# A two-layer hybrid decoder trunk: causal mask added by VectorE in query rows 1 to 3, and the next layer's opening placed in the TensorE order of the last rows

## The chip, the cores and the metric

The kernel runs on one core of a Trainium2 chip. The metric is the device time of one execution in microseconds (us). TensorE (PE in the rows) multiplies matrices, VectorE (DVE) does elementwise work and reductions, ScalarE (ACT) does activations and casts, GpSimd (POOL) does small work, and SyncE (SP) issues most DMAs.

## The reference, cut to what matters

A residual stream of 512 rows by 1024 columns goes through two layers. Each layer normalises it (RMSNorm), projects it to 4376 columns, runs three parallel groups (sparse attention with 8 heads, a linear recurrence, a convolution module), and adds their joint output projection back to the stream. A last RMSNorm closes the trunk. The part of the attention that the change touches is a softmax over all keys up to the query's own row:

```python
def rms_norm(x, g):
    y = xf * lax.rsqrt(jnp.mean(xf * xf, axis=-1, keepdims=True) + EPS)
    return (y * g.astype(jnp.float32)).astype(x.dtype)
...
ms = (ok[..., None] & (tok <= t[None, None, :, None, None]))[:, :, None]
ss = jnp.where(ms, ss, NEG)
ps = jax.nn.softmax(ss, axis=-1)
...
sw = jnp.einsum('bgrqd,bgkd->bgrqk', qb, kw).astype(jnp.float32) * scale
pw = jax.nn.softmax(jnp.where(mw, sw, NEG), axis=-1)
...
x = x + mixed @ w_out[l]
return rms_norm(x, final_g)
```

With 512 rows the "selected" branch takes every valid block and the window is as long as the sequence, so both branches are a causal softmax.

## The kernel before, in words

Rows are tiled by 128 into four tiles t = 0 to 3 (query row blocks i = 0 to 3). All products are made in split form: a value is held as a high part and a low part, and a product is the sum of high by high, high by low and low by high. `cast` writes a high part on ScalarE, `lower` subtracts it from the value on VectorE (tiles `whi`, `wlo`; `H` holds the turned, normalised stream in both parts).

**Opening of a layer.** For each tile the RMSNorm (`rms_norm`, in layer 0 the steps q, c, p of `START`), the turning of the result by TensorE transposes (`turned`, L271 to L274) and the projection to values and gates (L327, 24 matmuls of 280 columns for each tile). In layer 0 the order of ScalarE and VectorE is written out by hand in `START`: q is the square sum on ScalarE, c the inverse root on VectorE and GpSimd, p a product on VectorE, t a turning, w a part of the value weights. Then 384 and more projection matmuls follow without a break (L208).

**Attention, row blocks 2, 3 and 1** (`weights_of`, `turned_weights`, `values`). For each block there are eight heads and two branches; for i = 2 and 3 one call of `weights_of` handles one head and branch, for i = 1 two heads. A call writes scores to PSUM (L779, L780), adds the mask by a third matmul of `identb` and `maskb` (L781), finds the row minimum of the negated scores on VectorE (L784), takes the exponential on ScalarE from PSUM to `P` with a row sum (L787), inverts the sum (L789), scales `P` on GpSimd (L791). `turned_weights` transposes `P` on TensorE (L798), casts it on ScalarE (L800) and takes the low part on VectorE (L801); `values` multiplies it by the values (L813). PSUM buffers: three named `ps` for scores, two named `pt` for transposes, two named `acc`. `P` has four buffers in SBUF. The order of every engine outside the manual blocks is made by a scheduler. It puts the 96 matmuls of `out_proj(X, 8, MC)` (L423 with `mch`, `mcl`), which depend on nothing in the attention, between the attention's own matmuls; they are called fillers below.

**Last rows** (`last_rows`). Row block 0 and the 96 matmuls of the last part of the output projection run on TensorE in the order of `LAST_ROWS`: s scores, t turning, c and d the compressed branch, o and v the value products, r30 for example the output rows of tile 3, column half 0, added to the stream `X` by VectorE (L425). The opening of the next layer comes after them in the program, and the scheduler fills its instructions in.

**End.** The last RMSNorm writes `o` by tile, tile 0 last and in two halves, each with its own output DMA.

Of the kernel before, what the change touches and what calls it, by code (L numbers as in the profile page):

```python
# [1 line left out]

# [45 lines left out]
def tile_hybrid_trunk(ctx, tc, x_in, positions, norm_g, w_in, b_gate, cmp_pos, cmp_w1, cmp_w2, lru_conv_w,  # L48
# [30 lines left out]
    maskb = const.tile([128, 128], BF16, name="maskb")  # L79
# [132 lines left out]
    def rsqrt(y, v4):  # L212
# [706 lines left out]
    for l in range(DEPTH):  # L919
        X = layer(l, X)  # L920
# [34 lines left out]
```

## Time and profile before

| | |
|---|---|
| median of 3 runs | 786.5 us (785.53 to 787.01) |
| the profiled execution's own time | 786.09 us |
| its span, first to last instruction | 784.3 us |
| instructions | 10943 |
| PE busy (matmul) | 755.0 us, 96% |
| DVE busy | 676.4 us, 86% |
| ACT busy | 452.1 us, 58% |
| POOL busy | 101.7 us, 13% |
| mean granted TensorE clock | 0.997 |

The span leaves 1.8 us of the execution's time outside. Busy shares are means over stages that differ; a matmul's end is modelled, so consecutive matmuls overlap in the rows and the distance from start to start is what one costs.

### The profile page before, as it was taken

How to read it: one execution, taken by the hardware profiler on the slowest of the kernel's cores; microseconds unless marked ns; L12 is line 12 of the kernel's file. 1: busy time of each engine (PE TensorE's matmuls, PEld its weight loads, DVE VectorE, ACT ScalarE, POOL GpSimd, SP SyncE). 2: the span in 40 equal slices, each digit the busy share in tenths (PEclk: the TensorE clock that was granted, in tenths of full speed). 3: DMA queues.
4: the chain of work that ended last, by engine and by line, in shares of the span. 5: the costliest groups of instructions: out<-in, count | busy, mean ns of one | idle time of the engine just before them, and what ended most of it. 6: DMA issues, size and time to landing. Idle time of an engine off the chain costs nothing.

```text
span 784.3 us, 10943 instructions
## 1 busy us (share of the span) xinstructions
PE 755.0 (96%) x3816; PEld 604.8 (77%) x3816; DVE 676.4 (86%) x1243; ACT 452.1 (58%) x889; POOL 101.7 (13%) x179
## 2 busy tenths in 40 slices
PE   6999999999999999999989999999999999999995
PEld 4988887677887777888788888776788787778874
DVE  5889999999997788978873999999999778888766
ACT  5443666784336466667642348669534466676663
POOL 2000000000001132433210000000000103434240
PEclk9999999999999999999999999999999999999998
DMA  6433285656432200103531334771854140010002
GB/s 192 155 108 107 57 223 133 167 164 222 142 128 81 81 2 1 54 1 86 169 105 54 107 89 126 188 199 32 275 165 160 53 145 17 1 55 2 1 28 107
DMA packets 68245, 82.01 MB, mean 105 GB/s; under 512 B 6601, under 2 KB 56841, under 8 KB 68190
## 3 DMA queue, kind: packets, MB, share of 16 engines
q1 hardware_dynamic: 68190, 81.31, 33.9%
q8 instruction: 30, 0.49, 0.3%
q14 instruction: 25, 0.20, 0.1%
HBM read 67.67 MB, written 4.19 MB: 92 GB/s over the span
## 4 chain that ended last, share of the span: by engine, by line
PE 78%; DVE 9%; ACT 6%; issue 4%; POOL 2%; DMA 0%; POOLq 0%; DVEq 0%; SPq 0%; ACTq 0%
PE acc L208 43%; PE acc L423 10%; PE po L813 5%; PE pt L798 3%; PE acc L718 3%; PE acc L327 3%; PE ps L779 2%; ACT P L787 2%; PE ps L780 2%; DVE wlo L153 1%; DVE cv L381 1%; PE pt L630 1%; POOL P L791 1%; ACT pt L800 1%; PE pt L735 1%
## 5 line engine op out<-in xcount | busy, mean ns | idle before, releaser
L208 PE MATMUL acc<-H,whi 128*128 128x512 f32 x1024 | 325.5, 398 | 0.0
L208 PEld LDWEIGHTS acc<-H,whi 128*128 128x128 f32 x1024 | 191.1, 188 | 47.5 <-issue 1.9
L208 PE MATMUL acc<-H,wlo 128*128 128x512 f32 x512 | 203.7, 399 | 2.1 <-DVE wlo L153 2.1
L150 ACT CAST whi<-raw 128x1024 fp32r<-128x1024 f32 x102 | 106.5, 1050 | 159.4 <-PE acc L208 130.1
L381 DVE SCALAR_TENSOR_TENSOR cv<-sg,dww,cv 128x493 f32<-128x493 f32 (+18 forms) x240 | 165.9, 737 | 0.9
L153 DVE TENSOR_TENSOR wlo<-raw,whi 128x1024 fp32r<-128x1024 f32 x102 | 124.8, 1225 | 22.1 <-ACT whi L150 21.2
L208 PEld LDWEIGHTS acc<-H,wlo 128*128 128x128 f32 x512 | 96.2, 188 | 27.3 <-DVE wlo L153 3.4
L791 POOL TENSOR_SCALAR P<-P,hm,gt 128x384 f32<-128x384 f32 (+3 forms) x128 | 81.1, 643 | 135.7 <-DVE hm L789 127.1
L787 ACT ACTIVATE P<-ps,hm 128x384 f32<-128x384 f32 (+3 forms) x128 | 67.0, 532 | 15.7 <-DVE hm L784 15.1
L801 DVE TENSOR_TENSOR pt<-pt 128x512 fp32r<-128x512 f32 (+1 forms) x88 | 54.2, 638 | 12.9 <-ACT pt L800 11.8
L784 DVE TENSOR_REDUCE hm<-ps 128x1 f32<-128x384 f32 (+3 forms) x88 | 54.8, 634 | 8.2 <-PE ps L781 4.4
L813 PE MATMUL po<-pt,vv 128*128 128x256 f32 (+1 forms) x304 | 58.0, 304 | 1.1 <-DVE pt L801 0.7
L215 POOL TENSOR_TENSOR mv<-mv,power 128x1 f32<-128x1 f32 x8 | 4.2, 544 | 418.1 <-DVE mv L680 418.1
L800 ACT CAST pt<-pt 128x512 fp32r<-128x512 f32 (+1 forms) x88 | 46.0, 548 | 21.4 <-PE pt L798 18.8
L813 PEld LDWEIGHTS po<-pt,vv 128*128 128x128 f32 x304 | 44.7, 189 | 9.8 <-ACT pt L800 4.6
L798 PE MATMUL pt<-ident,P 128*128 128x128 f32 x320 | 47.6, 275 | 1.6 <-POOL P L791 1.3
L779 PE MATMUL ps<-KH,QS 128*128 128x384 f32 (+3 forms) x128 | 45.5, 367 | 0.8 <-ACT P L787 0.6
L798 PEld LDWEIGHTS pt<-ident,P 128*128 128x128 f32 x320 | 36.9, 140 | 6.0 <-POOL P L791 4.1
L780 PE MATMUL ps<-KL,QS 128*128 128x384 f32 (+3 forms) x128 | 40.5, 328 | 0.0
L327 PE MATMUL acc<-wv,H 128*128 128x280 f32 x192 | 30.6, 313 | 2.5 <-ACT wv L150 1.5
L425 DVE TENSOR_TENSOR x<-x,acc 128x512 f32<-128x512 f32 x48 | 32.4, 677 | 0.8 <-PE acc L423 0.4
L423 PE MATMUL acc<-whi,mn 128*128 128x512 f32 x96 | 31.1, 406 | 0.0
(233 smaller groups left out, 1213.3 us busy)
## 6 DMA issues: line engine op xcount, KB each, us to landing
raw<-in_w_in_dram SPq DMA_DIRECT2D x30, 1024.0 KB
raw<-in_w_out_dram SPq DMA_DIRECT2D x12, 1024.0 KB
raw<-in_cmp_w_dram SPq DMA_DIRECT2D x8, 1024.0 KB
x<-in_x_dram SPq DMA_DIRECT2D x8, 512.0 KB
raw<-in_w_in_dram SPq DMA_DIRECT2D x4, 512.0 KB
QS<-rs SPq DMA_DIRECT2D x8, 256.0 KB
QS<-ru SPq DMA_DIRECT2D x8, 256.0 KB
KH<-rs SPq DMA_DIRECT2D x8, 256.0 KB
```

The costliest lines, as they stand in the source:

```text
L150: S.copy(out, in_)
L153: (eng or V).tensor_tensor(out, in_, hi.bitcast(F32), op=OP.subtract)
L208: PE.matmul(p, w[k], h[k], start=n == 0, stop=n == 23)
L381: V.scalar_tensor_tensor(a[:, s:], u[:, :T - s], dww[:, ct, j:j + 1], a[:, s:], op0=OP.mult, op1=OP.add)
L423: PE.matmul(p, h[:, k], w, start=m == 0, stop=m == 11)
L779: PE.matmul(sc[:, r, :], q, KH[g][:, b, :L], start=r == 0, stop=False)
L780: PE.matmul(sc[:, r, :], q, KL[g][:, b, :L], start=False, stop=False)
L784: V.tensor_reduce(hm[:, 0, :nh], sc, axis=AX.X, op=OP.min)
L787: S.activation(P[:, r * L:(r + 1) * L], sc[:, r, :], AF.Exp, scale=-1.0, bias=hm[:, 0, r:r + 1], accum_out=hm[:, 1, r:r + 1])
L791: G.tensor_scalar(P[:, r * L:(r + 1) * L], P[:, r * L:(r + 1) * L], hm[:, 2, r:r + 1], GA[i][:, h0 + r, 1 + b:2 + b], op0=OP.mult, op1=OP. ...
L798: PE.transpose(pt[:, kb, :], P[:, kb * 128:(kb + 1) * 128], ident)
L813: PE.matmul(po, v, PT[w][:, kb].rearrange("p r q -> p (r q)"), start=False, stop=last and kb == i and w == 1)
```

## The change

Three things change. In row blocks 1 to 3 the mask matmul goes, and one VectorE instruction for each head adds the mask (now a bf16 tile of 512 columns, zero but for its last 128) to the scores, writes the sum to `P` and finds the minimum; the exponential then reads `P`. Row block 0 keeps the matmul. The opening of the next layer becomes an object whose steps (L loads, W value weights, N norm, T turning, V values) stand in `LAST_ROWS`, within the hand-written TensorE order. In `START` the inverse root is cut in two (c and e), the value weights come in three loads instead of two, their parts stand earlier, and the DMA of `norm_g` moves from SP's queue to ScalarE's. In `rms_norm` the tile that comes last takes its second half first, multiplies it by the gain early on VectorE and scales it on ScalarE. The small tiles `pos` and `hid` share buffers of other tiles.

```diff
-LAST_ROWS = "s10 c s00 r30 s01 r20 d r10 t00 o0 t01 s11 v00 v01 r21 t10 t11 r31 o1 v10 v11 r11 r01 r00"
-START = "q3 c3 p30 p31 q2 t30 c2 t31 p20 w0 p21 q1 t20 c1 w1 t21 p10 q0 p11 w2 t10 c0 t11 p00 p01 t00 t01"
+LAST_ROWS = "s10 c s00 r30 s01 r20 d r10 t00 o0 t01 s11 v00 v01 r21 L N2 t10 W t11 r31 N3 o1 v10 v11 T2 r11 N1 r01 " \
+            "T3 r00 N0 V2 T1 V3 T0 V1 V0"
+START = "q3 c3 e3 p30 p31 q2 c2 w0 e2 t30 p20 t31 q1 p21 c1 w1 e1 t20 p10 t21 q0 p11 c0 w2 e0 t10 p00 t11 p01 t00 t01"
...
-    maskb = const.tile([128, 128], BF16, name="maskb")
+    mask = const.tile([128, 512], BF16, name="mask")
+    maskb = mask[:, 384:]
...
+    G.memset(mask[:, :384], 0.0)
...
-        for n in range(2):
+        for n in ((1, 0) if last else (0, 1)):
             S.activation(y[:, n], x[:, n], AF.Square, accum_out=ss[:, n:n + 1])
...
+                if last:
+                    V.tensor_tensor(y[:, 1], x[:, 1], gb[:, 1], op=OP.mult)
...
-        for n in (slice(0, 1), slice(1, 2)) if halves else (slice(0, 2),):
-            V.scalar_tensor_tensor(y[:, n], x[:, n], ss[:, 2:3], gb[:, n], op0=OP.mult, op1=OP.mult)
+        n = slice(0, 1 if last else 2)
+        V.scalar_tensor_tensor(y[:, n], x[:, n], ss[:, 2:3], gb[:, n], op0=OP.mult, op1=OP.mult)
+        if last:
+            S.activation(y[:, 1], y[:, 1], AF.Copy, scale=ss[:, 2:3])
...
+        load_x(0, X, (3,))
+        grow = pair("grow")[0:1].rearrange("p a c -> p (a c)")
+        S.dma_start(out=grow, in_=norm_g[0:1, :])
+        load_x(0, X, (2,))
+        load_wv(0, 3)
+        load_wv(3, 3)
+        load_x(0, X, (1, 0))
+        load_wv(6, 2)
+        load_bg()
...
-                    PE.matmul(sc[:, r, :], q, KL[g][:, b, :L], start=False, stop=False)
-                PE.matmul(sc[:, :, L - 128:], identb, maskb.unsqueeze(1).to_broadcast([128, nh, 128]),
-                          start=False, stop=True)
+                    PE.matmul(sc[:, r, :], q, KL[g][:, b, :L], start=False, stop=i > 0 and r == nh - 1)
                 hm = work.tile([128, 3, 4], F32, name="hm", tag="hm", bufs=8)
-                V.tensor_reduce(hm[:, 0, :nh], sc, axis=AX.X, op=OP.min)
                 P = big("P", tag="P")
+                if i == 0:
+                    PE.matmul(sc, identb, maskb.unsqueeze(1).to_broadcast([128, nh, 128]), start=False, stop=True)
+                    V.tensor_reduce(hm[:, 0, :nh], sc, axis=AX.X, op=OP.min)
                 for r in range(nh):
-                    S.activation(P[:, r * L:(r + 1) * L], sc[:, r, :], AF.Exp, scale=-1.0,
-                                 bias=hm[:, 0, r:r + 1], accum_out=hm[:, 1, r:r + 1])
+                    p = P[:, r * L:(r + 1) * L]
+                    if i:
+                        V.tensor_tensor_reduce(p, sc[:, r, :], mask[:, 512 - L:], 1.0, BIG, OP.add, OP.min,
+                                               hm[:, 0, r:r + 1])
+                    S.activation(p, p if i else sc[:, r, :], AF.Exp, scale=-1.0, bias=hm[:, 0, r:r + 1],
+                                 accum_out=hm[:, 1, r:r + 1])
...
-        last_rows(X)
-        return X
+        return X, last_rows(X)
```

**VectorE in the middle of row block 3.** `TENSOR_REDUCE hm<-ps` is the minimum of one call, `RECIPROCAL hm` its inverse row sum, `pt<-pt` the low part of a turned block. Before:

```order
452 L801 TENSOR_TENSOR pt<-pt 128x4x128
453 L789 RECIPROCAL hm<-hm 128x1
454 L784 TENSOR_REDUCE hm<-ps 128x1
455 L801 TENSOR_TENSOR pt<-pt 128x4x128 x2
456 L789 RECIPROCAL hm<-hm 128x1 x2
457 L153 TENSOR_TENSOR wlo<-raw,whi 128x1024
458 L801 TENSOR_TENSOR pt<-pt 128x4x128 x2
459 L789 RECIPROCAL hm<-hm 128x1
460 L784 TENSOR_REDUCE hm<-ps 128x1 x2
```

The same place with the change; `ISA P,hm<-ps,mask` is the new instruction, and `ISA hm` behind it brings the minimum out:

```order
474 L847 TENSOR_TENSOR pt<-pt 128x4x128
475 L835 RECIPROCAL hm<-hm 128x1
476 L831 ISA P,hm<-ps,mask 128x512
477 L831 ISA hm 128x1
478 L847 TENSOR_TENSOR pt<-pt 128x4x128 x2
479 L835 RECIPROCAL hm<-hm 128x1
480 L831 ISA P,hm<-ps,mask 128x512
481 L831 ISA hm 128x1
```

Each minimum of one instruction is now two, and the order around them is otherwise alike.

**TensorE at the end of row block 1.** `acc<-wlo,mch` is a filler, `pt<-ident,P` a transpose of row block 1's `P`, `po<-pt,vv` its value products, and the 128-column `ps` rows are row block 0's scores. The first row of each piece is the layer's last filler. Before:

```order
1455 L423 MATMUL acc<-wlo,mch 128x512
1456 L779 MATMUL ps<-KH_1075,QS_725 128x128
1457 L780 MATMUL ps<-KL_1077,QS_725 128x128
1458 L779 MATMUL ps<-KH_1075,QS_726 128x128
1459 L780 MATMUL ps<-KL_1077,QS_726 128x128
1460 L805 MATMUL po<-ct,vcz 128x512
1461 L813 MATMUL po<-pt,vv 128x256 x8
1462 L798 MATMUL pt<-ident,P 128x128
1463 L813 MATMUL po<-pt,vv 128x256
1464 L798 MATMUL pt<-ident,P 128x128 x3
```

Now:

```order
1374 L463 MATMUL acc<-wlo,mch 128x512
1375 L819 MATMUL ps<-KH_1079,QS_729 128x128
1376 L859 MATMUL po<-pt,vv 128x256 x3
1377 L844 MATMUL pt<-ident,P 128x128 x4
1378 L820 MATMUL ps<-KL_1081,QS_729 128x128
1379 L819 MATMUL ps<-KH_1079,QS_730 128x128
1380 L820 MATMUL ps<-KL_1081,QS_730 128x128
1381 L819 MATMUL ps<-KH_1079,QS_729 128x128
1382 L844 MATMUL pt<-ident,P 128x128 x4
```

The last filler now stands ahead of 12 transposes of `P` (two groups of four are shown, a third follows six rows later) where 4 were left before.

**TensorE between the two layers.** `acc<-whi,mn` and `acc<-wlo,mn` are the last output rows (r00), `pt<-ident,hnat` transposes of the next layer's normalised stream, `acc<-wv,H` its value products. Before:

```order
1614 L423 MATMUL acc<-wlo,mn_3534 128x512
1615 L271 MATMUL pt<-ident,hnat 128x128 x6
1616 L327 MATMUL acc<-wv,H_3868 128x280
1617 L271 MATMUL pt<-ident,hnat 128x128 x4
1618 L327 MATMUL acc<-wv,H_3870 128x280
1619 L327 MATMUL acc<-wv,H_3868 128x280
1620 L271 MATMUL pt<-ident,hnat 128x128 x4
```

Now the transposes of tiles 2 and 3 stand ahead of r00, and 24 value products come directly behind it, with tile 1's transposes after them:

```order
1533 L463 MATMUL acc<-wlo,mn_3506 128x512
1534 L307 MATMUL acc<-wv,H_3508 128x280
1535 L307 MATMUL acc<-wv,H_3510 128x280
1536 L307 MATMUL acc<-wv,H_3508 128x280 x2
1537 L307 MATMUL acc<-wv,H_3510 128x280
1538 L307 MATMUL acc<-wv,H_3508 128x280 x2
```

Transposes of one tile and value products of another now alternate in whole blocks of 8 and 24 (V2, T1, V3, T0, V1, V0), where the two were mixed row by row.

## Rows read from the trace of the kernel before

**Rows 1.** The page's chain of work that ended last, by engine.

```profile
PE 78%; DVE 9%; ACT 6%; issue 4%; POOL 2%; DMA 0%; POOLq 0%; DVEq 0%; SPq 0%; ACTq 0%
```

**Rows 2.** Stretches: length, each engine's busy us (instructions), TensorE clock, DMA share, GB/s.

```profile
5.93:27.92 21.99, 17.72 (x107) 16.40 (x107) 17.15 (x44) 13.65 (x24) 2.29 (x4) 1.00 0.65 206
266.00:362.00 96.00, 93.87 (x588) 75.59 (x588) 79.84 (x185) 65.74 (x175) 34.46 (x51) 1.00 0.07 21
393.12:414.06 20.94, 18.61 (x142) 17.33 (x140) 13.66 (x32) 9.75 (x21) 2.04 (x4) 1.00 0.25 79
```

**Rows 3.** Chain in order of time: start us, length us, what.

```profile
31.59 89.79 PE acc L208 x384
...
329.80 0.87 PE pt L798 x8
...
405.37 8.16 PE acc L327 x63
414.12 89.79 PE acc L208 x384
```

**Rows 4.** TensorE's timeline in row block 3: start us, length us, instruction.

```profile
318.84 0.23 PE L781 MATMUL ps<-maskb,identb 128*128 128x128 bf16 x1
318.88 0.48 PE L779 MATMUL ps<-KH,QS 128*128 128x512 f32 x1
319.19 0.28 PE L813 MATMUL po<-pt,vv 128*128 128x256 f32 x1
```

**Rows 5.** Groups by line and shape, whole run: count | busy us, mean ns | idle before.

```profile
L801 DVE TENSOR_TENSOR pt<-pt 128x512 fp32r<-128x512 f32 x56 | 37.3, 687 | 7.8 <-ACT pt L800 7.3
L787 ACT ACTIVATION_READ_ACCUMULATOR P<-ps,hm 128x1 f32 x128 | 26.2, 205 | 0.0
L784 DVE TENSOR_REDUCE hm<-ps 128x1 f32<-128x512 f32 x32 | 21.3, 682 | 4.8 <-PE ps L781 2.6 <-PE acc L423 1.9
L784 DVE TENSOR_REDUCE hm<-ps 128x2 f32<-128x512 f32 x16 | 10.8, 683 | 0.4 <-PE ps L781 0.4
L545 DVE TENSOR_TENSOR_SCAN xc<-xc,rg 128x512 f32<-128x512 f32 x8 | 9.6, 1222 | 0.0
...
L789 DVE RECIPROCAL hm<-hm 128x1 f32<-128x1 f32 x64 | 9.2, 153 | 1.7 <-ACT P L787 1.5
...
L332 DVE TENSOR_TENSOR vv<-acc,vv 128x256 fp32r<-128x256 f32 x8 | 3.4, 420 | 3.1 <-ACT vv L331 3.1
```

**Rows 6.** Two such inversions back to back, VectorE's timeline in row block 3.

```profile
323.58 0.21 DVE L789 RECIPROCAL hm<-hm 128x1 f32<-128x1 f32 x2
```

**Rows 7.** TensorE's timeline at the border of the layers.

```profile
386.00 0.62 PE L423 MATMUL acc<-whi,mn 128*128 128x512 f32 x2
...
396.23 0.40 PE L327 MATMUL acc<-wv,H 128*128 128x280 f32 x1 [0.89 <-ACT H L273]
397.88 0.66 PE L271 MATMUL pt<-ident,hnat 128*128 128x128 f32 x4 [1.25 <-DVE H L274]
```

**Rows 8.** VectorE's timeline there: tile 0's last addition and its norm.

```profile
395.40 0.68 DVE L425 TENSOR_TENSOR x<-x,acc 128x512 f32<-128x512 f32 x1
...
400.73 0.15 DVE L228 SCALAR_TENSOR_TENSOR ss<-ss 128x1 f32<-128x1 f32 x1
```

**Rows 9.** The start, timeline: DMA issue of x on SP's queue, tile 0's last low parts.

```profile
1.20 0.83 SPq L111 DMA_DIRECT2D x<-in_x_dram  x2
...
26.54 1.38 DVE L274 TENSOR_TENSOR H<-pt,H 128x512 fp32r<-128x512 f32 x2
```

**Rows 10.** Groups of VectorE by line from 5.9 to 28 us.

```profile
L217 DVE SCALAR_TENSOR_TENSOR nw<-ss,nw 128x1 f32<-128x1 f32 x4 | 0.9, 220 | 1.4 <-POOL ss L215 1.4
```

**Rows 11.** The end, VectorE's timeline for tile 0.

```profile
778.46 0.15 DVE L227 TENSOR_SCALAR ss<-ss 128x1 f32<-128x1 f32 x1 [0.79 <-ACT o L225]
...
779.93 1.42 DVE L231 SCALAR_TENSOR_TENSOR o<-x,ss,g 128x512 f32<-128x512 f32 x2
```

More of the change, by code (lines that the diff above doesn't have):

```diff
@@ L1 @@
 from contextlib import ExitStack
+from types import SimpleNamespace
 import concourse.bass as bass
@@ L253, in chan, with layer @@
+    def layer(l, X, o):
+        Hh, Hl, VV, GT = o.Hh, o.Hl, o.VV, o.GT
         def chan(name, src2d, n):
@@ L261, in chan @@
             return t
-        H2 = [[quad(f"H{w}{a}") for a in range(2)] for w in range(2)]
-        Hh, Hl = [[H2[w][k // 4][:, k % 4, :] for k in range(8)] for w in range(2)]
-        WV = [None] * 8
-        def turned(t, h, n):
-            p = psum.tile([128, 4, 128], F32, name="pt", tag="tr", bufs=2)
-            for k in range(4):
-                PE.transpose(p[:, k, :], h[:, n, k * 128:(k + 1) * 128], ident)
-            sl = slice(t * 128, (t + 1) * 128)
-            S.copy(H2[0][n][:, :, sl], p)
-            V.tensor_tensor(H2[1][n][:, :, sl], p, H2[0][n][:, :, sl].bitcast(F32), op=OP.subtract)
@@ L287, in layer @@
-        if l == 0:
-            hs, ss = {}, {}
-            gp = [psum.tile([128, 512], F32, name="acc", tag="ps", bufs=3) for n in range(2)]
-            for n in range(2):
-                PE.matmul(gp[n], one, grow[:, n * 512:(n + 1) * 512], start=True, stop=True)
-            def squares(t):
-                hs[t] = pair("hnat")
-                ss[t] = work.tile([128, 4], F32, name="ss", tag="ss", bufs=4)
-                S.activation(hs[t], X[t], AF.Square, accum_out=ss[t][:, 0:1])
-            def chain(t):
-                V.tensor_scalar(ss[t][:, 3:4], ss[t][:, 0:1], 4.0 / DM, 4.0 * EPS, op0=OP.mult, op1=OP.add)
-                rsqrt(ss[t][:, 2:3], ss[t][:, 3:4])
-            def product(t, n):
-                V.scalar_tensor_tensor(hs[t][:, n], X[t][:, n], ss[t][:, 2:3], gp[n], op0=OP.mult, op1=OP.mult)
-            steps = dict(q=squares, c=chain, p=product, t=lambda t, n: turned(t, hs[t], n), w=value_weights)
-            with tc.manual_schedule(engines={mybir.EngineType.Activation, mybir.EngineType.DVE}):
-                for step in START.split():
-                    steps[step[0]](*map(int, step[1:]))
-        else:
-            for j in range(3):
-                value_weights(j)
-            for t in (2, 3, 1, 0):
-                SP.dma_start(out=saved[t], in_=X[t])
-                h = rms_norm(X[t], gb, "hnat", t == 0)
-                for n in range(2):
-                    turned(t, h, n)
@@ L589, in do_prep @@
         def do_prep(c):
-            pos = work.tile([16, 128], F32, name="pos", tag="pos", bufs=1)
+            pos = work.tile([16, 128], F32, name="pos", tag="oe", bufs=1)
             SP.dma_start(out=pos, in_=cmp_pos[l, c].rearrange("(j s) d -> j (s d)", s=2))
@@ L637, in do_main @@
                           stop=True)
-            hid = work.tile([128, 2, 64], F32, name="hid", tag="hid", bufs=1)
+            hid = work.tile([128, 2, 64], F32, name="hid", tag="m")
             S.activation(hid, ph, AF.Tanh, scale=0.5)
@@ L884, in last_rows @@
                     steps = dict(s=soft, t=turn, c=comp, d=turn_comp, o=open_po, v=vals, r=rows)
+                    if nxt:
+                        steps |= nxt.steps
                     for step in LAST_ROWS.split():
-                        steps[step[0]](*map(int, step[1:]))
+                        if step[0] in steps:
+                            steps[step[0]](*map(int, step[1:]))
+                return nxt
             return last_rows
@@ L914, in layer @@
         out_proj(X, 8, MC)
-        last_rows(X)
-        return X
+        return X, last_rows(X)
     X = [None] * 4
+    o = opening(0, X)
     for l in range(DEPTH):
-        X = layer(l, X)
+        X, o = layer(l, X, o)
     gb = load_g(final_g)
```

135 lines of the change are left out of this document (90 added, 45 removed).

## The prediction

> **What bounds the kernel now.** I read the chain of waits first: three quarters and more of what ended last is TensorE's own work [rows 1]. So time can come from TensorE work that goes away, or from stretches in which it waits. I then read the windows, and they show three such places [rows 2]. From 5.93 to 27.92 us, the opening of layer 0, VectorE is busy 17.15 of 21.99 us: neither engine is full, each waits for the other. From 266 to 362 us, row blocks 2, 3 and 1 of layer 0, TensorE is busy 93.87 of 96.00 us and VectorE 79.84. From 393.12 to 414.06 us, the border of the layers, neither is full. Everything between (the long runs of L208 [rows 3]) is a stream of matmuls at 89.79 / 384 = 0.234 us each, which the change doesn't touch: what is won ahead of it is passed on whole, since layer 1's first run, with no opening of layer 0 behind it, takes the same 89.79 us.
>
> **The attention stage, what goes.** Each call of `weights_of` in row blocks 1 to 3 loses a mask matmul: 16 + 16 + 8 = 40 a layer. Its price is read from starts: the mask matmul is followed after 0.04 us by the next score matmul, which then holds the one after it off for 0.31 us [rows 4], where 0.234 is the rule [rows 3]. So 0.04 + 0.08 = 0.12 us a call, 40 x 0.12 = 4.8 us of TensorE a layer. [...]
>
> **What comes in its place.** VectorE's minimum of one call (682 ns for 512 columns) becomes an instruction over the same columns with a PSUM and an SBUF source, whose nearest row is the low part of L801, 687 ns [rows 5]: no difference. In row block 1 one minimum over two heads (683 ns) becomes two of 256 columns, nearest row 420 ns: 8 x (0.840 - 0.683) = 1.3 us a layer, with the small differences 1.4. Then there is the instruction that brings each minimum out, 16 + 16 + 16 = 48 a layer, which no row of VectorE shows. Below: the second of two inversions back to back adds 0.21 - 0.153 = 0.06 us [rows 5, 6]. Above: ScalarE's own read of an accumulator, 205 ns [rows 5]. I take 0.12, between the two, because the new one can't start before the sum behind it is complete, so it hides less than an independent inversion. That makes 1.4 + 48 x 0.12 = 7.2 us of VectorE a layer (4.3 to 11.2).
>
> [...]
>
> What lies beside it: the stage's TensorE need falls from 96.0 to 91.2 us. VectorE's sum rises from 79.84 to 87.0, 95% of that. At 83% its lateness cost TensorE the 2.1 us that it stood idle. At 95%, in one fixed order, with only three score buffers, two transpose buffers and four `P`, more of the chain minimum, exponential, inversion, scaling, transpose, low part comes late. One place shows it: the last filler now stands ahead of 12 transposes of row block 1 instead of 4, so two more groups end without cover. Such a group costs VectorE a low part of 0.687 and TensorE only 0.87 / 2 = 0.435 for four transposes [rows 3, 5]; with the cast between them I price the two at 1 us each less what overlaps, 1.5 us. For the rest of the stage I take another 1.6. Net 4.8 - 3.1 = 1.7 us a layer, 3.4 in both. For the other parts of a call I put nothing: the exponential reads SBUF instead of PSUM on an engine busy 65.74 of 96 us [rows 2], and scores' PSUM buffers come free earlier, by about an exponential.
>
> **The border of the layers.** From 386.00 (r11) [rows 7] to the first projection matmul at 414.12 [rows 3] there are 28.12 us. The work in it: 36 output matmuls at 0.234 (8.4), 30 transposes at 0.87 / 8 = 0.109 (3.3), 96 value products at 8.16 / 63 = 0.130 (12.5), 8 narrow transposes at no more than 0.109 (0.9): 25.0 us. So 3.1 us are waiting, of which the two waits named in the rows (0.89 and 1.25) are the largest part [rows 7]; they end with VectorE's low part and ScalarE's cast of a turned tile. In the new order each turning has a block of other matmuls behind it: T2 has r11 and r01 (24 x 0.234 = 5.6 us), T3 has r00, T1 has V3 (24 x 0.130 = 3.1). What is late next is tile 0's norm. Before, VectorE added its last rows at 395.40 and came to its first norm step at 400.73 [rows 8], held off by other tiles' work in its queue. Now 24 + 24 products and T1's 8 transposes, 7.1 us, lie between r00 and T0, and VectorE's order puts two weight low parts and one low part of tile 1 in between; I count about 6 us for the norm, so the cover holds by 1 us. The steps' DMAs (L) stand on SP's queue where they stood. I take 2.7 us, between 1.2 (one wait stays) and 3.1.
>
> **The start.** The first x is issued at 1.20, behind the DMA of `norm_g`, and one issue takes 0.83 / 2 = 0.4 us [rows 9]; that DMA moves to another queue: 0.4 us earlier. Cutting c in two puts other work into three of four waits for GpSimd's root, 1.4 x 3 / 4 = 1.0 us [rows 10]. Of VectorE's remaining idle time (4.84 - 1.0 = 3.8 [rows 2]) I let the new order recover 1.7, nearly half. VectorE then ends tile 0's low parts 3.1 us before 27.92 [rows 9]. But 48 value products now stand behind tile 0's transposes instead of 34, 14 x 0.130 = 1.8 us. Net 1.3 us; from 0.4 (only the issue) to 0.4 + 4.84 - 1.8 = 3.4. The memset of the wider mask is hidden: GpSimd has nothing due until the first root at 6 us.
>
> **The end.** Tile 0's two halves stand one behind the other on VectorE, 1.42 us [rows 11]; one goes to ScalarE, 0.7 us, and one small step of 0.15 leaves the chain. The two output DMAs still are issued one after the other, so I take 0.7, between 0.4 and 0.9.
>
> **Sum.** 3.4 + 2.7 + 1.3 + 0.7 = 8.1 us off the profiled execution's 786.09: 778.0 us. That execution lies 0.4 us under the median of the runs, so the median may come out as much later. 0.2% (1.6 us) is about what a measurement of this kernel can tell from no change.
>
> **Rivals.**
> *VectorE takes all that TensorE gives.* For it: 87.0 of 91.2 us leaves nearly no slack, and at 205 ns a read VectorE's sum is 91.1, as much as TensorE's. Against it: much of VectorE's idle time before was waiting for TensorE, which it can do without. Then only 4.7 us come, from the other three parts: 781.4 us.
> *VectorE becomes the bound and the stage is longer than before.* This is the case on the slower side. VectorE can't be fuller than its chain lets it; if a quarter of its 16 idle us must stay (4 us), the stage takes 79.84 + 1.4 + 48a + 4, a being all that a minimum costs more than now. It is as long as before, 96, at a = 0.22, and it eats the other 4.7 us too at a = 0.22 + 2.35 / 48 = 0.27. At a = 0.35 it takes 102.0, 6.0 more in each layer: 786.1 - 4.7 + 12.0 = 793.4 us. A row that speaks for it is the scan of 512 columns, which carries a value along and takes 1222 ns [rows 5]: if the new instruction ran at that rate, VectorE would grow by some 20 us a layer more, and the time would be about 810 us. Against it: the minimum carries a value too, at 682 ns.
> *TensorE's saving comes whole.* For it: the scheduler laid its fillers anew, and score buffers come free sooner. 786.1 - 4.7 - 9.6 = 771.8 us.
> *The border keeps its wait.* Tile 0's norm is late by more than its 1 us of cover, since VectorE's queue held it off by 5 us before [rows 8]; 2.2 of the 2.7 us go: 780.2 us.
>
> **How the numbers follow.** Forecast 0.40; VectorE takes all 0.23; the saving comes whole 0.13; the border keeps its wait 0.12; VectorE as the bound 0.12, of which a quarter falls short of being slower. The first four are all faster by more than 1.6 us. Faster 0.87, same 0.04, slower 0.09. The range reaches from the whole saving with a better start (771.8 less 1) up to the point where VectorE's price has eaten the other parts: 770.8 to 786.2 us. The forecast's own range, with the four parts' bounds taken half way, is 774 to 782.
>
> **What would show it.** In the new profile: the new instruction near 0.69 us for 512 columns and its read near 0.1 (0.2 or more: VectorE is the bound); VectorE above 90% in the stage, and TensorE's idle time there 4 to 6 us; the distance from r11 to the first projection matmul of layer 1 near 24.8 us (28.1 - 2.7, and six transposes that now stand ahead of r11); the first projection matmul of layer 0 at 30.3; tile 0's last step on VectorE 0.75 us long. What would make the prediction wrong: a read that costs more than 0.2 us, a new instruction slower than 0.8, or value products that wait behind T0 at either opening.

## The result, and the profile after

The changed kernel takes 776.6 us (median of 4 runs, 775.51 to 776.74) against 786.0 (785.39 to 787.01): ratio 0.988, 95% interval 0.9865 to 0.9894. The profiled execution is the fastest one, 775.51 us with a span of 773.7 and a mean granted clock of 0.997; the other three had 0.993. Against the profiled execution of before that is 10.6 us less. The prediction was 778.0.

Two rows of the page of the kernel after: busy time of each engine, and the chain by engine.

```profile
PE 744.1 (96%) x3736; PEld 603.3 (78%) x3736; DVE 678.3 (88%) x1355; ACT 456.8 (59%) x891; POOL 105.7 (14%) x180
...
PE 76%; DVE 10%; ACT 6%; issue 3%; DMA 2%; POOL 2%; SPq 0%; POOLq 0%; DVEq 0%; ACTq 0%
```

TensorE is busy 10.9 us less than before and its share of the chain falls by 2 points [rows 1]. VectorE, which was given the work, is busy only 1.9 us longer. To see where the time went I cut both executions at the same matmuls of TensorE's timeline. The table holds all kernels, the experiments below too (us; a column is the distance between two starts in TensorE's timeline of the profiled execution).

| kernel | median | profiled | clock | start | fill 0 | tail 0 | border | fill 1 | tail 1 | last rows | end |
|---|---|---|---|---|---|---|---|---|---|---|---|
| before | 786.0 | 786.1 | 0.997 | 232.3 | 90.76 | 7.24 | 51.06 | 90.65 | 7.25 | 31.56 | 7.40 |
| after | 776.6 | 775.5 | 0.997 | 232.2 | 84.20 | 10.99 | 46.94 | 84.16 | 10.99 | 30.61 | 7.43 |
| e1 | 782.9 | 782.2 | 0.990 | 231.7 | 84.16 | 13.27 | 51.65 | 84.15 | 11.49 | 30.58 | 7.39 |
| e2 | 784.5 | 784.0 | 0.995 | 231.5 | 88.87 | 8.24 | 51.57 | 88.87 | 8.27 | 31.15 | 7.38 |
| e3 | 779.9 | 781.4 | 0.996 | 232.4 | 83.77 | 12.25 | 51.05 | 83.77 | 12.26 | 30.61 | 7.38 |
| e4 | 777.8 | 778.5 | 0.993 | 234.2 | 84.23 | 11.57 | 46.94 | 84.00 | 11.72 | 30.60 | 7.46 |
| e5 | 778.4 | 779.5 | 0.989 | 231.5 | 84.21 | 13.27 | 48.54 | 84.48 | 11.44 | 30.62 | 7.44 |
| e6 | 774.1 | 774.1 | 0.997 | 232.5 | 90.42 | 3.34 | 47.44 | 90.43 | 3.35 | 31.14 | 7.44 |
| e7 | 783.0 | 784.4 | 0.998 | 233.6 | 90.86 | 7.23 | 47.85 | 90.75 | 7.23 | 31.56 | 7.43 |
| e8 | 774.9 | 774.9 | 0.997 | 232.1 | 83.04 | 11.86 | 46.95 | 83.10 | 11.86 | 30.61 | 7.43 |
| e9 | 771.5 | 772.9 | 0.998 | 231.4 | 90.45 | 3.35 | 47.42 | 90.38 | 3.34 | 31.13 | 7.45 |
| e10 | 776.7 | 780.9 | 0.987 | 233.9 | 84.14 | 13.26 | 48.40 | 84.16 | 11.42 | 30.61 | 7.26 |
| e11 | 777.1 | 777.5 | 0.995 | 231.9 | 90.37 | 3.35 | 51.64 | 90.44 | 3.33 | 31.11 | 7.40 |
| e12 | 771.2 | 771.1 | 0.997 | 230.2 | 90.45 | 3.34 | 47.39 | 90.38 | 3.34 | 31.12 | 7.01 |

"Start" runs to the first matmul of the output projection's part `mlh`, with layer 0's opening and projections in it; "fill" from a layer's first score matmul to its last filler; "tail" from there to r30; "border" from r30 of layer 0 to the first matmul of layer 1's long run of projections; "last rows" from r30 of layer 1 to TensorE's last end, "end" the rest of the span. What is left out is the same everywhere: 32.6 to 32.7 us between start and fill 0, and 233.4 to 233.6 us between border and fill 1 (the projections of layer 1).

So the 10.6 us come from the attention (2.8 in layer 0, 2.75 in layer 1), the border (4.1) and the last rows (0.95); start and end give 0.1 together, and layer 1's projections take 0.2 back. Windows of the fill and the tail of layer 0, before (length; busy us of TensorE, weight loads, VectorE, ScalarE, GpSimd; clock; DMA):

```profile
265.00:355.76 90.76, 89.32 (x556) 71.43 (x555) 74.00 (x176) 62.74 (x170) 34.46 (x51) 1.00 0.04 14
355.76:363.00 7.24, 6.55 (x50) 5.85 (x49) 7.15 (x11) 4.72 (x11) 0.00 (x0) 1.00 0.42 121
```

and after:

```profile
264.80:349.00 84.20, 83.00 (x505) 69.56 (x504) 73.27 (x225) 62.04 (x164) 32.31 (x47) 1.00 0.05 16
349.00:359.99 10.99, 8.23 (x63) 7.06 (x62) 9.74 (x19) 8.42 (x23) 4.80 (x7) 1.00 0.31 92
```

In the fill TensorE is idle 90.76 - 89.32 = 1.4 us before and 1.2 after: it waits no longer there than it did. In the tail it is idle 0.7 before and 2.8 after. TensorE's timeline there, after (start, length, instruction, idle time ahead of it):

```profile
349.00 0.48 PE L463 MATMUL acc<-wlo,mch 128*128 128x512 f32 x1
...
351.70 0.39 PE L825 MATMUL ps<-mask,identb 128*128 128x512 bf16 x1
353.83 0.97 PE L844 MATMUL pt<-ident,P 128*128 128x128 f32 x4 [1.74 <-POOL P L837]
...
357.12 0.74 PE L859 MATMUL po<-pt,vv 128*128 128x256 f32 x4 [0.61 <-DVE pt L847]
...
359.99 0.81 PE L463 MATMUL acc<-whi,mn 128*128 128x512 f32 x2
```

The last filler is at 349.00. At 351.70 TensorE has nothing left, waits 1.74 us for GpSimd's last `P`, and once more 0.61 us for a low part. In before TensorE's longest wait in the stage was 0.56 us; fillers still stood in row block 1 then.

VectorE's new instruction, by groups (count, busy us, mean ns, idle time before), to be set beside the plain minimum of 682 ns and the inversions [rows 5]:

```profile
L831 DVE CUSTOM_DVE_ANT_0 P<-ps,mask 128x512 f32<-128x512 f32 x32 | 21.5, 678 | 2.4 <-PE pt L844 2.2
...
L831 DVE CUSTOM_DVE_ANT_0 P<-ps,mask 128x256 f32<-128x256 f32 x32 | 12.4, 417 | 4.7 <-PE pt L844 4.1 <-POOL P L837 0.6
...
L831 DVE DVE_READ_ACCUMULATOR2_ANT hm<- 128x1 f32 x96 | 7.9, 82 | 0.0
```

And the place where its price shows, VectorE's timeline in row block 3. The first row is two plain minima of the kernel before, the others are after:

```profile
316.74 1.27 DVE L784 TENSOR_REDUCE hm<-ps 128x1 f32<-128x512 f32 x2
...
317.03 0.67 DVE L831 CUSTOM_DVE_ANT_0 P<-ps,mask 128x512 f32<-128x512 f32 x1
317.62 0.08 DVE L831 DVE_READ_ACCUMULATOR2_ANT hm<- 128x1 f32 x1
317.62 1.50 DVE L158 TENSOR_TENSOR wlo<-raw,whi 128x1024 fp32r<-128x1024 f32 x1
...
319.72 0.08 DVE L831 DVE_READ_ACCUMULATOR2_ANT hm<- 128x1 f32 x1
319.72 1.28 DVE L847 TENSOR_TENSOR pt<-pt 128x512 fp32r<-128x512 f32 x2
```

The next instruction starts in the same moment as the 0.08 us read behind it (317.62, 319.72). New instruction and read together hold the queue for 0.59 us here, start to start, and for 0.60 in the median of the 32 of this size; a plain minimum of 512 columns also holds it for 0.60.

The border after, TensorE's timeline:

```profile
382.66 0.71 PE L463 MATMUL acc<-whi,mn 128*128 128x512 f32 x2
...
388.31 1.04 PE L280 MATMUL pt<-ident,hnat 128*128 128x128 f32 x8
389.11 0.71 PE L463 MATMUL acc<-whi,mn 128*128 128x512 f32 x2
...
391.99 3.29 PE L307 MATMUL acc<-wv,H 128*128 128x280 f32 x24
395.12 1.04 PE L280 MATMUL pt<-ident,hnat 128*128 128x128 f32 x8
395.91 3.39 PE L307 MATMUL acc<-wv,H 128*128 128x280 f32 x24
399.14 1.04 PE L280 MATMUL pt<-ident,hnat 128*128 128x128 f32 x8
399.93 6.48 PE L307 MATMUL acc<-wv,H 128*128 128x280 f32 x48
...
406.93 0.50 PE L213 MATMUL acc<-H,whi 128*128 128x512 f32 x1
```

No row of it has a wait: from r11 (382.66) to 406.93 there are 24.27 us, and in a stretch from 386 to 407 TensorE is busy 21.00 of 21.00. Before, the same distance was 28.06 with two waits named [rows 7].

### The profile page after: what moved, and what is told of

Read it like the earlier page. It is cut to its first block, busy times and chain, and to the rows that moved or that the text cites. A ratio compares the mean times of both kernels' runs of the same rounds, so it can differ in the third digit from the quotient of the medians.

```text
span 773.7 us, 10853 instructions
## 1 busy us (share of the span) xinstructions
PE 744.1 (96%) x3736; PEld 603.3 (78%) x3736; DVE 678.3 (88%) x1355; ACT 456.8 (59%) x891; POOL 105.7 (14%) x180
## 4 chain that ended last, share of the span: by engine, by line
PE 76%; DVE 10%; ACT 6%; issue 3%; DMA 2%; POOL 2%; SPq 0%; POOLq 0%; DVEq 0%; ACTq 0%
PE acc L213 44%; PE acc L463 11%; PE po L859 4%; PE pt L844 3%; PE acc L758 3%; PE acc L307 3%; PE ps L819 2%; PE ps L820 2%; DVE cv L421 1%; ACT P L833 1%; PE pt L670 1%; ACT pt L846 1%; POOL P L837 1%; DVE wlo L158 1%; DMA nat<-in_conv_dw_w_dram 1%
## 5 line engine op out<-in xcount | busy, mean ns | idle before, releaser
L837 POOL TENSOR_SCALAR P<-P,hm,gt 128x384 f32<-128x384 f32 (+3 forms) x128 | 83.5, 660 | 125.3 <-DVE hm L835 118.5
L833 ACT ACTIVATE P<-P,hm 128x384 f32<-128x384 f32 (+2 forms) x96 | 59.0, 616 | 10.2 <-DVE hm L831 9.6
L831 DVE CUSTOM_DVE_ANT_0 P<-ps,mask 128x384 f32<-128x384 f32 (+2 forms) x96 | 51.5, 548 | 11.1 <-PE pt L844 7.2
L859 PE MATMUL po<-pt,vv 128*128 128x256 f32 (+1 forms) x304 | 56.2, 301 | 2.5 <-DVE pt L847 1.9
L844 PEld LDWEIGHTS pt<-ident,P 128*128 128x128 f32 x320 | 36.9, 140 | 10.9 <-POOL P L837 7.8
L819 PE MATMUL ps<-KH,QS 128*128 128x384 f32 (+3 forms) x128 | 42.5, 345 | 0.0
L465 DVE TENSOR_TENSOR x<-x,acc 128x512 f32<-128x512 f32 x48 | 32.6, 679 | 1.3 <-PE acc L463 1.1
```

The source lines that it names most:

```text
L819: PE.matmul(sc[:, r, :], q, KH[g][:, b, :L], start=r == 0, stop=False)
L833: S.activation(p, p if i else sc[:, r, :], AF.Exp, scale=-1.0, bias=hm[:, 0, r:r + 1], accum_out=hm[:, 1, r:r + 1])
L837: G.tensor_scalar(P[:, r * L:(r + 1) * L], P[:, r * L:(r + 1) * L], hm[:, 2, r:r + 1], GA[i][:, h0 + r, 1 + b:2 + b], op0=OP.mult, op1=OP. ...
L844: PE.transpose(pt[:, kb, :], P[:, kb * 128:(kb + 1) * 128], ident)
L859: PE.matmul(po, v, PT[w][:, kb].rearrange("p r q -> p (r q)"), start=False, stop=last and kb == i and w == 1)
```

## The experiments

Each set ran on one chip beside the kernel before, whose medians there are 786.0 us for e1 to e4, 786.2 for e5 to e8, 785.3 for e9 to e11 and 785.4 for e12. A ratio is to the kernel before, with its 95% interval.

**e1 to e3: the two halves of the mask change.** In each layer the change takes a matmul from TensorE and gives VectorE and ScalarE new work. On the kernel before, e1 makes the whole mask change, e2 keeps a third matmul, e3 makes neither half (no mask).

```diff
 # e1: weights_of, the mask tile and the places of pos and hid as after; all else as before
 # e2: e1, and behind the scores of rows 1 to 3
+                if i:
+                    PE.matmul(sc[:, :, L - 128:], identb, mask[:, :128].unsqueeze(1).to_broadcast([128, nh, 128]),
+                              start=False, stop=True)
 # e3: before, with the third matmul in row block 0 alone, and the places of pos and hid as after
+                if i == 0:
+                    PE.matmul(sc, identb, maskb.unsqueeze(1).to_broadcast([128, nh, 128]), start=False, stop=True)
```

> The kernel before with the mask change alone (the small tiles pos and hid moved, to make room for the wider mask). Theory: the attention stages gained 2.5 to 2.9 us a layer between the two traces, and this has nothing to do with the border or the start: 786.0 - 5.3 = 780.7 us (780.0 to 781.4). The prediction's own term (1.7 a layer) gives 782.6. Rival: part of the stage's gain comes from the last rows and the new opening, which the scheduler lays beside it: 783 us or more.

> As e1, but TensorE's third matmul of every call stays in rows 1 to 3, now with zeros, so that TensorE does its old work and VectorE its new. Theory (the mask matmul is worth 4.8 us of TensorE a layer, and VectorE's extra work costs TensorE about 2.2 of them by lateness): 780.7 + 9.6 = 790.3 us. [...]

> The kernel before without the mask in rows 1 to 3: no mask matmul, the old minimum, the exponential from PSUM (it leaves out the causal mask of the diagonal blocks). Theory (4.8 us a layer, all of it on the path when VectorE does no more than before): 786.0 - 9.6 = 776.4 us. [...] If it is no faster than e1, VectorE's extra work costs nothing.

Measured: e1 782.9 us (782.2 to 783.7; ratio 0.9963, 0.9948 to 0.9977), e2 784.5 (0.9977, 0.9968 to 0.9987), e3 779.9 (0.9931, 0.9912 to 0.9951). No theory's number was met: e1 came 2.2 us over its 780.7, e2 5.8 under its 790.3, e3 3.5 over its 776.4. e1 came within 0.3 of the prediction's own term (782.6), by luck, as its windows below show, and near its rival's 783, for a reason that this did not name. Fill and tail together, where the clock was full, give a square: before 98.0 us a layer, e3 96.0, e2 97.1, after 95.2. Taking the matmul out is worth 2.0 us with the old minimum (98.0 to 96.0) and 1.9 with the new instruction (97.1 to 95.2). The new instruction is worth another 0.8 to 0.9 us by itself, a gain, in both rows of the square. So on balance VectorE's extra work costs the stage nothing, against the prediction and against my theory for e2. By the sign that e3's expectation named (e3 no faster than e1) it would cost something, since e3's median is 3.0 us lower; but e1's trace shows the clock lost in both layers' tails, as shown below, and e3's does not. And e3's tail, without any new work on VectorE:

```profile
348.80:361.05 12.25, 9.97 (x77) 8.85 (x76) 9.93 (x18) 9.51 (x28) 5.91 (x9) 1.00 0.28 76
```

It is idle 12.25 - 9.97 = 2.3 us, nearly as long as after's 2.8. So the hole behind the last filler opens without any new work on VectorE: with less of its own work in the fill, TensorE runs through the fillers 6 to 7 us earlier. How much of the other 0.5 us is VectorE's these three runs don't show; in e2, whose fill is only 1.9 us shorter, the tail's idle time is 1.6 us. Why the new instruction gains 0.85 I did not settle: the exponential then reads `P`, so a score buffer is free one exponential earlier, and the one wait of a score matmul for an exponential (0.3 us in before's stage) is gone in e2, which is a third of it.

e1 was expected at 780.7 and shows what else the hole does. Its windows in 5 us, where the column behind GpSimd's busy time is the granted clock:

```profile
350.00:355.00 5.00, 2.98 (x21) 2.29 (x21) 4.65 (x9) 3.04 (x7) 1.95 (x3) 0.98 0.17 39
355.00:360.00 5.00, 4.59 (x23) 4.29 (x21) 3.81 (x7) 3.54 (x10) 2.32 (x3) 0.50 0.48 142
360.00:365.00 5.00, 5.00 (x18) 4.34 (x17) 3.99 (x12) 2.84 (x12) 1.20 (x3) 0.50 0.53 157
365.00:370.00 5.00, 5.00 (x27) 4.18 (x27) 2.73 (x6) 2.41 (x10) 1.73 (x4) 0.99 0.00 0
```

TensorE does 2.98 us of work in the first window; behind it the clock is at 0.50 for some ten microseconds. Its tail takes 13.27 us where the same order took 10.99 at full clock. The tail of layer 1 (11.49) has a stretch at 0.50 too, from 737.1 to 740.6 us. All six runs of e1 show 0.988 to 0.990.

**e4 and e5: why the start gained nothing.** VectorE's timeline after, in the opening of layer 0 (the two VectorE instructions of tile 0's step c, L352 and L221, with a step of the rope tables between them, and the last low part of the value weights):

```profile
17.15 0.15 DVE L352 TENSOR_SCALAR ss<-ss 128x1 f32<-128x1 f32 x1
19.32 0.43 DVE L131 CAST ang<-pi 128x512 f32<-128x512 int32 x1 [2.02 <-DMA pi<-in_positions_dram]
19.67 0.15 DVE L221 TENSOR_SCALAR nw<-ss 128x1 f32<-128x1 f32 x1
19.73 0.73 DVE L158 TENSOR_TENSOR wv<-raw,wv 128x560 fp32r<-128x560 f32 x1
```

The scheduler put the cast of the positions inside step c, where it stands 2.02 us for its load, which SyncE issues at 14.93; behind it wait the rest of tile 0's root and the weights. Before, that cast came after 22 us and waited for nothing.

```diff
 # e4: the loads of inv and pi moved from rope_tables to the opening, behind load_x(0, X, (1, 0))
+        o.pos = load_positions()
         load_wv(6, 2)
 # e5: no load moved
-            rope_tables()
+            with tc.issue_after(o.last[1].ins):
+                rope_tables()
```

> The kernel with the whole change, but the two loads of the positions and the frequencies stand on SyncE's queue ahead of the last value weights, not behind the eleven small loads of the convolution's parameters. Theory: the 2.02 us that VectorE waits at the cast of the positions, in the hand-written order of the opening, go; TensorE's later waits (0.76 for the weights' low part, 0.63 for tile 0) shrink, and the first run of projections starts about 1.5 us earlier: 775.1 us (774.6 to 775.8). Rival: the cast hides waits that come anyway (the weights and tile 0 arrive as late as before): 776.6 us, within 0.4.

> The kernel with the whole change, but the steps of the position tables are queued behind the last low part of the opening on VectorE; no load is moved. Theory (the cast that waits 2.02 us for the positions, in the middle of the opening, is what ate the start's gain): the cast is gone from there, the last weights' low part comes about 2 us earlier, the first long run of projections starts 1.2 to 1.8 us earlier: 776.6 - 1.5 = 775.1 us. Rival (tile 0's own chain or the weights' arrival ends as late without it): 776.6, within 0.4.

Measured: e4 777.8 us (0.9904, 0.9885 to 0.9923), e5 778.4 (775.1 to 780.7; 0.9902, 0.9882 to 0.9922). Both expectations missed. In e4 the scheduler moved the cast forward with its load, to a place where it waits 3.24 us (8.60 to 11.84): the start is 2.0 us longer; the clock fell besides (0.67 from 355 to 360 us, in the tail of layer 0), and the tails take 11.57 and 11.72 us. In e5 the cast is out of the way (26.00) and the start 0.6 us shorter, less than the 1.5 hoped for, since the next thing is late at once. ScalarE's timeline of e5, tile 0's two turned halves:

```profile
22.55 0.59 ACT L282 CAST H<-pt 128x512 fp32r<-128x512 f32 x1
23.04 1.05 ACT L155 CAST whi<-raw 128x1024 fp32r<-128x1024 f32 x1
23.98 0.59 ACT L282 CAST H<-pt 128x512 fp32r<-128x512 f32 x1
```

A weight cast of 1.05 us, for projections whose long run starts at 31.5, stands between them. And e5 as a whole is slower than after: the clock of its runs is 0.987 to 0.995, and in the profiled one it fell behind the hole of row block 1 (0.50 from 355 to 365 us, tail 13.27 us again). Its run at 0.995 took 775.1 us, the one at 0.987 780.7.

**e6: fillers kept for the hole.** The 12 matmuls of tile 0's second half are held back.

```diff
+                    with tc.issue_after(HELD[5].ins) if kt0 == 8 and n == 1 and t == 0 else nullcontext():
                         out_rows(X, t, n, W, [m[:, :, t * 128:(t + 1) * 128] for m in M])
 # HELD: the last transpose of each call in row block 1
```

> The kernel with the whole change, but the last 12 fillers of each layer (tile 0's second half) may be issued only behind the sixth group of row block 1's transposes. Theory: the change emptied the fillers 6.6 us earlier (last score to last filler 90.8 before, 84.2 after) and gave 3.75 of it back behind the last filler, where TensorE stands idle for some 2.8 us a layer; 12 x 0.234 = 2.8 us of fillers fit there. If half of them are not missed where they stood: 1.4 us a layer, 776.6 - 2.8 = 773.8 us (772 to 775), and the granted clock stays full there in every run. Rival (VectorE is the bound of the whole stage, so that a filler moved is an idle gap moved): 776.6, within 0.6.

Measured: 774.1 us (773.9 to 775.2; 0.9851, 0.9838 to 0.9864), near the 773.8 expected, but not by the terms expected. Fill and tail take 93.76 us a layer, 1.4 less than after's 95.19. The place of the hole, in windows:

```profile
350.00:355.00 5.00, 4.98 (x32) 3.86 (x30) 4.31 (x9) 4.36 (x10) 1.79 (x4) 1.00 0.00 0
355.00:360.00 5.00, 5.00 (x37) 4.63 (x36) 4.83 (x8) 3.89 (x11) 0.00 (x0) 1.00 0.88 272
```

TensorE is busy 9.98 of 10 us where after has 2.99 + 4.25, and the runs' clocks are 0.995 to 0.998. The last rows give 0.5 us back in each layer: in layer 1 they are the same 142 matmuls, but a wait of 0.26 us at `po<-ct,vcz`, 0.41 before and gone in after, is there again, which is half of it. So 0.9 us a layer is the net; the profiled executions of after and e6, both at 0.997, differ by 1.4 us, and the rest of the 2.5 between the medians goes with the clock.

**e7: everything but the mask.**

```diff
 # after, with weights_of as before (mask matmul, plain minimum, exponential from PSUM)
```

> The kernel with the whole change but the mask: rows 1 to 3 have the mask matmul and the plain minimum as before. Theory: the two traces give 4.1 us for last rows and border, 0.2 for the start and 0.9 for the end: 786.0 - 5.2 = 780.8 us. The prediction's own terms (2.7, 1.3, 0.7) give 781.3. Rival (the border's gain needs the mask change, whose scores leave buffers and engines free earlier): 783 us or more.

Measured: 783.0 us (782.7 to 785.2; 0.9969, 0.9957 to 0.9981): 3.3 off, not 5.2, which is the rival's number. The border takes 47.85 us, 3.2 less than before; the other 0.9 of after's 4.1 belong to the mask change, as does the gain in the last rows of layer 1 (31.56 here as in before, 30.61 in after). From r11 to the projections e7 takes 24.25 us, as after does, so that the 0.9 lies ahead of r11. In the profiled execution the cast of the positions waited 2.83 us and the start was 1.25 us longer than before.

**e8: row block 1 back on the mask matmul.**

```diff
-                if i == 0:
+                if i < 2:
...
-                    if i:
+                    if i > 1:
```

> The kernel with the whole change, but row block 1 has its mask matmul back (8 calls a layer, one minimum over two heads), rows 2 and 3 keep the new instruction. VectorE saves 8 x (2 x 0.417 + 2 x 0.082 - 0.683) = 2.5 us a layer there, TensorE gets 8 x about 0.15 = 1.2 us more. Theory (VectorE is late in row block 1, TensorE idle): net 0.6 to 1.3 us a layer less, 776.6 - 1.9 = 774.7 us. Rival (TensorE's work counts, VectorE's is hidden): 776.6 + 2.4 = 779.0 us.

Measured: 774.9 us (774.8 to 776.8; 0.9863, 0.9851 to 0.9876), the expected number, but only a part of it for the expected reason. Fill and tail are 94.90 us instead of 95.19; the profiled executions, both at 0.997, differ by 0.6 us. TensorE's idle time in the stage falls by 0.8 us and its busy time rises by 0.5, where 1.2 were estimated; this fits VectorE's new work costing TensorE something in row block 1, without proving it. The rest of the 1.7 between the medians goes with the clock: three of e8's four runs are at 0.997 or 0.998, three of after's four at 0.993. Whether that is e8's doing four runs each can't tell.

**e9, e11: repairs.** e9 is after with the fillers of e6, the tables of e5, and ScalarE's early weight casts behind tile 0's; e11 is e1 with the fillers of e6.

```diff
+        with tc.issue_after(o.last[0].ins) if l == 0 else nullcontext():
+            do_glu()
```

> The kernel with the whole change, the last 12 fillers of each layer held back as in e6, the position tables behind the opening on VectorE as in e5, and ScalarE's first casts of projection weights behind its last cast of the opening (one such cast of 1.05 us stood between tile 0's two). Theory: e6's 774.1, less 0.6 for the cast of the positions (as the traces of e5 show), less about 0.8 for the second cast of tile 0: 772.7 us (772 to 773.5), with a full clock in row block 1. Rival (the start stays bound by the loads): 774.1, within 0.4.

> e1 (the mask change alone) with the last 12 fillers of each layer held back as in e6. Theory: e1 loses its gain in one hole of TensorE in row block 1 and in the half clock behind it (its last filler to r30 takes 13.3 and 11.5 us, where 11.0 is the same at full clock); with the hole filled the clock stays full, and the mask change is worth 7 to 9 us by itself: 778.2 us (777.5 to 779). Rival (the clock's fall has another cause, or the fillers are missed where they stood): 781 us or more.

Measured: e9 771.5 us (771.3 to 772.9; 0.9824, 0.9812 to 0.9837), 1.2 us better than expected and below the range given; e11 777.1 (776.5 to 777.5; 0.9889, 0.9875 to 0.9904), 1.1 better than expected. The mask change alone is worth 3.1 us with the hole (e1) and 8.3 without it (the fillers were not held on the kernel before by themselves; its tails are idle 0.7 us each, so there was little to win there); in e11 the clock is full in the stage and falls only at the border, whose waits it still has (0.81 from 390 to 395 us, 0.85 from 395 to 400).

**e10, e12: the end.** VectorE's timeline after, at the end:

```profile
764.89 1.29 DVE L246 SCALAR_TENSOR_TENSOR o<-x,ss,g 128x1024 f32<-128x1024 f32 x1
...
766.16 0.68 DVE L242 TENSOR_TENSOR o<-x,g 128x512 f32<-128x512 f32 x1
766.76 0.68 DVE L465 TENSOR_TENSOR x<-x,acc 128x512 f32<-128x512 f32 x1
768.23 0.16 DVE L243 SCALAR_TENSOR_TENSOR ss<-ss 128x1 f32<-128x1 f32 x1 [0.79 <-ACT o L238]
...
769.50 0.75 DVE L246 SCALAR_TENSOR_TENSOR o<-x,ss,g 128x512 f32<-128x512 f32 x1
```

The product of tile 0's second half with the gain (766.16) stands ahead of the addition of its last rows, which TensorE has ready at 766.28: the addition starts at 766.76, 0.48 us late. In e10 it starts 0.03 us behind TensorE's end.

```diff
 # e10: the last normalisation as before
 # e12: e9, and
+                    with tc.issue_after(ADDED[0].ins) if name == "o" else nullcontext():
                         V.tensor_tensor(y[:, 1], x[:, 1], gb[:, 1], op=OP.mult)
```

> The kernel with the whole change, but the last normalisation as before (tile 0's two halves one behind the other on VectorE). Theory: from TensorE's last matmul to the end the traces show 7.35 us before and 7.42 with the change, so the end gained nothing and this is 776.6 us, within 0.4. The prediction's term (0.7 us on the path) gives 777.3; if the halves decide, up to 777.5.

> e9, with one instruction of the last normalisation moved: the early product of tile 0's second half with the gain (0.68 us on VectorE) stands behind the addition of tile 0's last output rows, not ahead of it. Theory: the end gained nothing because this product holds that addition off by about 0.5 us, as much as the split of the halves saves; behind the addition VectorE waits 0.79 us for ScalarE's square sum anyway. From TensorE's last matmul to the end 6.9 us instead of 7.4, the whole 771.45 - 0.5 = 770.95 us. Rival (the end is bound by the output transfers, which start no earlier): 771.45, within 0.2.

Measured: e10 776.7 us (775.2 to 780.9; 0.9894, 0.9876 to 0.9913), e12 771.15 (770.99 to 771.58; 0.9815, 0.9802 to 0.9829). By its median e10 is as after, but its runs spread over 5.7 us with the clock (0.987 to 0.996; in the profiled one it fell in the opening too, 0.66 from 25 to 30 us), so the distance decides: its end takes 7.26 us, after's 7.43 (7.40 in before; the expectation's 7.35 and 7.42 are off by the rounding of the span). In all traces the old end takes 7.26 to 7.40 us and the new 7.43 to 7.46: it brought nothing. The late addition is only half of it. From that addition to VectorE's last step the new end is 0.9 us shorter, so the step still ends 0.43 us earlier behind TensorE's end than before. But both halves are then ready at once, and SyncE issues their two transfers one behind the other, at 770.24 and 770.66 us, where before the first was issued at 780.74 and the second at 781.37, as its half became ready. e12's timeline:

```profile
762.37 0.69 DVE L468 TENSOR_TENSOR x<-x,acc 128x512 f32<-128x512 f32 x1
762.98 0.68 DVE L243 TENSOR_TENSOR o<-x,g 128x512 f32<-128x512 f32 x1
763.85 0.16 DVE L244 SCALAR_TENSOR_TENSOR ss<-ss 128x1 f32<-128x1 f32 x1 [0.19 <-ACT o L238]
```

The product now fills the wait for the square sum, of which 0.19 of 0.79 us is left; the end takes 7.01 us, 0.44 less than in e9. The median, on another chip, moves by 0.3 us, not 0.5, within the spread of the runs, so here too the distance decides. e12 is the fastest version: 14.2 us less than before, 5.4 less than the change.

## Why the prediction came close, step by step

| term | predicted | traces |
|---|---|---|
| attention, both layers | 3.4 | 5.6 |
| border | 2.7 | 4.1 |
| start | 1.3 | 0.2 |
| end | 0.7 | 0.0 |
| last rows of layer 1, projections of layer 1 | none | 0.95 - 0.2 |
| sum, profiled executions | 8.1 | 10.6 |
| sum, medians | 8.1 | 9.4 |

The mechanism of the border held, and the total was near, in part by luck: attention and border gave 3.6 us more than predicted, start and end 1.8 less.

**TensorE's price of the mask matmul** was near: its busy time in fill and tail falls from 95.87 to 91.23, 4.64 us where 4.8 were predicted. But that is the fall of both halves: in e3, without the matmuls and with the old minimum, it falls by 4.3, and between e2 and after by 3.5. In time the matmul is worth 1.9 to 2.0 us a layer as long as the hole stands (e1 to e3).

**VectorE's price** is the step that failed: "I take 0.12, between the two, because the new one can't start before the sum behind it is complete". That reason was an estimate of mine, and no run shows it: the read's row starts at 317.62, that of the new instruction ends at 317.70. The read is 82 ns long but takes no time of the queue: new instruction and read take 0.60 us start to start, a plain minimum 0.60. The bound of 0.06 from two inversions was itself too high, and 0 should have been in the range. VectorE's busy time grew by 1.9 us in the whole run, not 14.4. The trace has 96 reads for 96 new instructions.

**Lateness.** "For the rest of the stage I take another 1.6" measured -0.2: the fill has as little idle time as before. "Two more groups end without cover", 1.5 us, was the right place: the tail's idle time grew by 2.1. But its cause was put down to VectorE's price; e3 shows 1.6 of these 2.1 without any new work on VectorE, and with fillers held back (e6) the tail has no idle time at all. The fillers were spent too early. 4.64 + 0.24 - 2.07 = 2.81 us in layer 0, as measured.

**The border.** The mechanism held: each turning is covered, and the cover of tile 0's norm "holds by 1 us". VectorE's timeline after:

```profile
393.16 0.68 DVE L465 TENSOR_TENSOR x<-x,acc 128x512 f32<-128x512 f32 x1
...
397.55 0.74 DVE L246 SCALAR_TENSOR_TENSOR hnat<-x,ss,g 128x512 f32<-128x512 f32 x1
```

The norm is ready at 398.29, 5.1 us after the addition began (about 6 were counted), and T0 starts at 399.14. e7 gives 3.2 us for the order alone, beside 2.7 predicted: all the waiting that was counted (3.1) is gone. 0.9 more come with the mask change, which the prediction did not connect with the last rows. One row was misread: tile 0's first norm step on VectorE stood at 398.34 before, not at 400.73, so its queue held it off for some 3 us and not 5.

**The start.** "I let the new order recover 1.7" failed: a foreign cast was scheduled into the hand-written order and waited 2.02 us. The issue of x did come earlier, at 0.79 us against 1.20 [rows 9]. The 0.2 of the table is one execution against one: the five traces with the old start have 231.5 to 232.4 us, the five with the new start as it stands 232.1 to 233.9, so it gained nothing. Once the cast and one misplaced weight cast are out (e9, e12) the start is 0.9 and 2.1 us shorter than before; these two nearly equal starts differ by 1.2 us, and ScalarE waits 1.30 us for a load of value weights in one and 0.34 in the other.

**The end.** "One goes to ScalarE, 0.7 us" was costed without its other half: the product that prepares it stands ahead of the last addition (0.48 us), and two transfers that become ready together are issued 0.42 us apart.

**Rivals.** "VectorE takes all" and "VectorE becomes the bound" fall with e2 and e3. "The border keeps its wait" falls with after's rows, which have none. "The saving comes whole" did not come true either: 5.6 of 9.6 us, nearer the forecast's 3.4; but with the fillers held the mask change alone gives 8.3 (e11). What no rival named was the clock, which fell to 0.50 behind TensorE's hole in e1 and e5 and made them slower than their parts.

**The signs.** Met: the new instruction (0.68 us for 512 columns), its read (0.08), the distance from r11 to the projections (24.27, forecast 24.8), the last step of tile 0 (0.75), TensorE's idle time in the stage (4.0, at the edge of 4 to 6). Missed: VectorE is busy 83.0 of 95.2 us there, 87% and not above 90, and layer 0's run of projections starts at 32.02 and not at 30.3.

## What to carry to other kernels

The work taken from the bound engine shortened this stage by 2.8 us in layer 0, and by 4.2 where independent work was left to fill the waits at its end (e6; 0.5 of it went again in the last rows): look where the last filler stands, and hold some back. The hole behind it cost e1 twice, by a wait of 1.75 us and by a granted clock of 0.50 behind that (tail 13.27 us against 10.99); after, with a wait of 1.74, paid once. In a hand-written order, see what the scheduler may put between its steps, and which load that waits for (2.02 us here).

## What the runs showed of the hardware

The granted clock fell to 0.50 behind TensorE's idle stretch in row block 1, in some executions and not in others: the 561 matmuls of that stage stand in one and the same order in after, e1, e4, e5 and e10, and after's profiled execution has a wait of 1.74 us there and stays at 1.00, while e1, with a wait of 1.75, falls to 0.50 and has a tail 2.3 us longer, and e4, e5 and e10 fall too (to 0.67, 0.50 and 0.50 in windows of 5 us). Three of after's runs have a mean of 0.993 and take 1.0 to 1.2 us longer; where their clock fell no trace shows. The read of VectorE's accumulator, 82 ns long, starts together with the next instruction where that one has nothing to wait for, and takes no time of the queue. The exponential of 512 columns costs 725 ns from SBUF (after) where it took 692 from PSUM (before):

```profile
L787 ACT ACTIVATE P<-ps,hm 128x512 f32<-128x512 f32 x32 | 22.1, 692 | 4.9 <-DVE hm L784 4.8
...
L833 ACT ACTIVATE P<-P,hm 128x512 f32<-128x512 f32 x32 | 23.2, 725 | 4.5 <-DVE hm L831 4.5
```
